# A pooling, convolution and attention trunk on TensorE: three groups of side work issued later

## The chip, the cores and the metric

The kernel runs on one core of a Trainium2 chip. The metric is the device time of one execution in microseconds (us). The engines are called as in the profile: PE is TensorE's matrix multiply, DVE is VectorE, ACT is ScalarE, POOL is GpSimd, and SP is SyncE, which here only issues DMAs.

## The reference

Four residual layers with a normalization ahead of each, and a final normalization: pooling, gated convolution, latent attention, pooling. Sequence 512, width 1024, inner width 2048. The parts that the change touches:

```python
# pooling layer: windows 2, 4, 8, 16, one for each quarter of the channels
u, z = jnp.split(xn @ w_in, 2, axis=-1)
mean = (c - prev) / jnp.minimum(count_base, float(w))[None, :, None]   # c: running sum of u
pooled.append(mean - uf[:, :, g])
mixed = jnp.einsum('bsgc,gcd->bsgd', pooled, w_grp).reshape(B, S, D_INNER) * scale
return (mixed * jax.nn.silu(z)) @ w_out

# attention layer, 16 heads: a part of the query is turned by its position
q_rope = apply_rope(q[..., QK_NOPE_DIM:], cos[:, :, None, :], sin[:, :, None, :])
s = (einsum('bqhd,bkhd->bhqk', qn_b, k_nope) + einsum('bqhr,bkr->bhqk', qr_b, k_rope)) * ATTN_SCALE
```

where `apply_rope` makes of two halves x1, x2 the pair x1 cos - x2 sin, x2 cos + x1 sin.

## The kernel before

Activations lie with channels on the partitions and the 512 positions along the free dimension. Every float32 product is formed on PE from high and low parts (h, l) as three matmuls: h·h, h·l, l·h (`mm3`, and the lines L261 to L263). So each weight chunk `wr` that SP loads (128x1024, 512 KB) is converted to `wh` by ACT (L248), and DVE subtracts to get `wl` (L251); activations are split in the same way (`split`, L158 and L161).

Layers 0 to 2 run as a stream of jobs. A job is one weight chunk (24 matmuls of 512 columns) or a *pair* of chunks, which is formed by seven half-size products with sums of weights and sums of activations (`seven`, L423 and L429). For a pair, `prepare_pair` makes on ACT and DVE the parts ah/al, sh/sl, ch/cl and, after two more sums (L402, L403), th/tl. The matching sums of the normalized activations are the *forms* of `XNorm.forms`: for each two of the eight x tiles, ACT makes g, DVE four sums d (L366 to L369), ACT two conversions fh, DVE two subtractions fl (L385). Jobs of a layer come in the order of `ORDER`: u, z and m with a group and a number (u12 is the chunk 2 of group 1 that gives u), h0 and h1 the two halves of the output projection. In the pooling layers u and m jobs are chunks; of the z jobs, those of group 0 of layer 0 are two chunks each (z00a, z00b), the others are pairs. In layer 0, z10 is the first pair, and so the first to read forms.

Work other than matmuls is put into a table of positions: eight positions make one job, and a step at position p is issued between the matmuls of that eighth of the job. The table orders PE, DVE and ACT in the program's own order; POOL and the DMA queues follow the program's order too. The last pooling layer and the heads of attention are not placed by such a table: there a scheduler at build time orders the engines.

For u, `post_u` puts at position 0 a multiplication by the normalization's factor (u, L583) and on POOL one to four shifted additions (s, L620), at 12 the mean on DVE (L626 to L628: hd, s, s), at 14 the high part `plh` on ACT (L631), at 16 the low part `pll` on DVE (L634). The multiplied, gated result of m is E and O or sz (L664), split into yh and yl (L667, L670).

In attention a head h passes `scores` (PE s, L1021 to L1025; DVE a masked maximum, L1029; ACT the exponential, L1033; DVE the reciprocal; POOL p times it, L1035), then the next head's query and key projection (pq, pk and their splits q, k), the mixing of head h-1 with the values (po, O or E), and `turn_p`, which transposes p on PE (pj, L1048) and splits it (th, tl, L1051). The turned queries are made for a group of four heads at once: `qrope` projects two halves A and B, does six DVE operations (L985 to L990), splits the two results (qa, qb), and spreads them by 16 DMAs on SP over four tiles `qrs` (L996), one for each head. `extra` is called at five places of a head and issues the next group's values and rotary work at the (head in the group, place) of `VALUES_AT` and `ROTARY_AT`.

Nearly all 128x512 tiles come from one ring of 70 slots (`ut`, NU = 70); a new tile takes the slot of the one 70 before it and waits for its readers, DMAs included. PSUM has eight banks, taken in a ring as well (`ps`).

Of the kernel before, what the change touches and what calls it, by code (L numbers as in the profile page):

```python
# [13 lines left out]
ALU = mybir.AluOpType  # L14
# [27 lines left out]


VALUES_AT = ((0, 3), (2, 0), (2, 0))
ROTARY_AT = ((2, 1), (1, 1), (1, 1))
SPLIT_Y_FROM = 10


# [16 lines left out]
def trunk_kernel(ctx: ExitStack, tc: tile.TileContext, a):  # L65
    nc = tc.nc
# [12 lines left out]
    def ut(s, dt=F32, w=S):  # L79
        return up.tile([P, S + PAD], dt, tag="u", name=nm(s))[:, :w]  # L80
# [74 lines left out]
    def split(src, s, eng="act", w=S):  # L155
        h, l = ut(s + "h", F32R, w), ut(s + "l", F32R, w)
        if eng == "act":
            nc.scalar.activation(h, src, AF.Copy)  # L158
        else:
            nc.vector.tensor_copy(h, src)  # L160
        nc.vector.tensor_tensor(out=l, in0=src, in1=f(h), op=ALU.subtract)  # L161
        return h, l
# [92 lines left out]
    def wchunk(src, width=CH, pool=False):  # L255
        w, steps = prepare_chunk(load_chunk(src, width)[0], width, pool)
        Steps(steps)(2)
        return w
# [323 lines left out]
    def tmul(dst, src, R):  # L582
# [1 line left out]


    LATE = "u20 u21 m10 u22 u23 m11 h0 z20 z21 u30 u31 m20 u32 u33 m21 z30 z31 m30 m31 h1"
    ORDER = ("u00 u01 u02 u03 u10 u11 u12 u13 z00 z01 m00 m01 z10 z11 " + LATE,
             "u00 u01 u02 u03 z00 z01 u10 u11 m00 u12 u13 m01 z10 z11 " + LATE)

    def pool_layer(stream, j, xn, half, mid=None, at=(1, 3), pre=None):  # L590
# [12 lines left out]
        for g, w in enumerate(WINDOWS):  # L603
            pooled, szs = [], []

            def post_u(t, sign, g=g, w=w, pooled=pooled):
                u = up.tile([P, S + PAD], F32, tag="u", name=nm("u"))
                h, l = ut("plh", F32R), ut("pll", F32R)
                pooled.append((h, l))
                sums = []  # L610

                def mul():
                    nc.gpsimd.memset(u[:, :PAD], 0.0)
                    tmul(u[:, PAD:], t, ly.R[sign])
                    sums.append(u)

                def add(d):
                    cur, nx = sums[0], up.tile([P, S + PAD], F32, tag="u", name=nm("s"))
                    lo = 2 * d - 1
                    nc.gpsimd.tensor_tensor(out=nx[:, lo:], in0=cur[:, lo:], in1=cur[:, lo - d : S + PAD - d], op=ALU.add)  # L620
                    sums[0] = nx

                def mean():
                    cur, pd = sums[0], sums[0][:, PAD:]
                    hd = sp.tile([P, PAD], F32, tag="hd", name=nm("hd"))
                    nc.vector.tensor_tensor(out=hd, in0=cur[:, PAD : 2 * PAD], in1=con[:, C_INV + PAD * g : C_INV + PAD * (g + 1)], op=ALU.mult)  # L626
                    nc.vector.scalar_tensor_tensor(out=pd, in0=cur[:, PAD:], scalar=1.0 / w, in1=u[:, PAD:], op0=ALU.mult, op1=ALU.subtract)
                    nc.vector.tensor_tensor(out=pd[:, :PAD], in0=hd, in1=u[:, PAD : 2 * PAD], op=ALU.subtract)  # L628

                def high():  # L630
                    nc.scalar.activation(h, sums[0][:, PAD:], AF.Copy)  # L631

                def low():
                    nc.vector.tensor_tensor(out=l, in0=sums[0][:, PAD:], in1=f(h), op=ALU.subtract)  # L634

                adds = [lambda q=q: add(2**q) for q in range(g + 1)]
                return {0: [mul, *adds], 12: [mean], 14: [high], 16: [low]}

            def post_z(t, sign, szs=szs, plain=g == 0 and pre is not None):
                sz = ut("sz") if plain else t  # L640

                def scale():
                    tmul(sz, t, ly.R[sign])

                def gate():
                    nc.scalar.activation(sz, sz, AF.Silu)
                    szs.append(sz)

                return {0: [scale], 3: [gate]}

            def mix(mm, g=g, pooled=pooled, szs=szs):
                def run(wl, now):
                    for e in range(2):
                        i = 2 * mm + e
                        pm = ps("pm")
                        for k in range(4):
                            now(4 * e + k)
                            c = slice(k * 2 * P + e * P, k * 2 * P + (e + 1) * P)
                            mm3(pm, wl[0][:, c], wl[1][:, c], *pooled[k], first=k == 0, last=k == 3)
                        y, h, l = szs[i], ut("yh", F32R), ut("yl", F32R)  # L660
                        ys[g // 2].append((h, l))

                        def gated(pm=pm, y=y, i=i):
                            nc.vector.scalar_tensor_tensor(out=y, in0=pm, scalar=pcol(f"pool_scale{j}", 4 * g + i), in1=y, op0=ALU.mult, op1=ALU.mult)  # L664

                        def high(h=h, y=y):
                            nc.scalar.activation(h, y, AF.Copy)  # L667

                        def low(h=h, l=l, y=y):
                            nc.vector.tensor_tensor(out=l, in0=y, in1=f(h), op=ALU.subtract)  # L670

                        (stream.later if e else now).put({0: [gated], 3: [high], 4: [low]} if e else {5: [gated], 6: [high], 7: [low]})

                stream.add(CHUNK, wg[g, mm], run)

            for i in range(4):
                u_[g, i] = lambda g=g, i=i, post_u=post_u: ly.tile(stream, wu[4 * g + i], post_u)
            for i in range(2):
                z_[g, i] = lambda g=g, i=i, post_z=post_z: (ly.pair if g or pre is None else two_tiles)(stream, wz[2 * g + i], (post_z, post_z), mid and mid(g, i))
                m_[g, i] = lambda mix=mix, i=i: mix(i)  # L680
            if g == 0 and pre is not None:
                u_[0, 0] = lambda post_u=post_u: stream.add(None, None, lambda w, now: ly.done(stream, *[(post_u, t, 1) for t in pre()]))
                u_[0, 1] = lambda: None
# [115 lines left out]
    def mla_layer(stream, xn, begin, cos_sin, nxt):  # L799
# [161 lines left out]
        def values(g):  # L961
            wh, wl = wchunk(wv[g])
            for tk in range(NT):
# [7 lines left out]
                    nc.tensor.matmul(pv, xl[:, ts_], wh[:, c], start=False, stop=(k == 1))  # L971
                vs[g, tk] = split(pv, "v")

        def qrope(g):
            wh, wl = wchunk(wq[8 + g], 768)
            ab = []
            for e in range(2):
                pa = ps("pa")
                mtile(pa, wh, wl, ql, kn=3, ktot=3, stride=2 * P, off=e * P)
                t = ut("qr")  # L980
                nc.scalar.activation(t, pa, AF.Copy)
                ab.append(t)
            A, B = ab
            t1, t2 = ut("t1"), ut("t2")
            nc.vector.tensor_tensor(out=t1, in0=A, in1=cos, op=ALU.mult)  # L985
            nc.vector.tensor_tensor(out=t2, in0=B, in1=sin, op=ALU.mult)
            nc.vector.tensor_tensor(out=t1, in0=t1, in1=t2, op=ALU.subtract)
            nc.vector.tensor_tensor(out=t2, in0=B, in1=cos, op=ALU.mult)
            nc.vector.tensor_tensor(out=A, in0=A, in1=sin, op=ALU.mult)
            nc.vector.tensor_tensor(out=t2, in0=t2, in1=A, op=ALU.add)  # L990
            parts = [*split(t1, "qa"), *split(t2, "qb")]
            order = [parts[0], parts[2], parts[1], parts[3]]
            for hh in range(4):
                st = ut("qrs", F32R)
                for q, src in enumerate(order):
                    nc.sync.dma_start(f(st)[32 * q : 32 * q + 32, :], f(src)[32 * hh : 32 * hh + 32, :])  # L996
                qrs[4 * g + hh] = st
# [74 lines left out]
        cos, sin = cos_sin  # L1072
        for h in range(H):
            g, e = divmod(h, 4)

            def extra(pos):
                if g < 3:
                    if (e, pos) == VALUES_AT[g]:
                        values(g + 1)
                    if (e, pos) == ROTARY_AT[g]:  # L1080
                        qrope(g + 1)

            extra(0)
            scores(h)
            extra(1)
            if h + 1 < H:
                stage_a(h + 1)
            extra(2)
            if h:
                mix(h - 1)  # L1090
            extra(3)
            if h >= SPLIT_Y_FROM:
                for _ in range(2):
                    split_y()
            if h + 1 == H:
                nxt.begin()
                nxt.step()
            turn_p(h)
            extra(4)
# [23 lines left out]
    def first_two():  # L1123
# [32 lines left out]
            s1.later.put({0: [lambda m=m: xn0.st.add(xt[m])]})  # L1156
        s1.later.put({3: [xn0.st.close]})
        for kk in range(KK):
            s1.later.put(xn0.forms(kk), 48 + 8 * kk)
        return pre  # L1160

    pool_layer(s1, 0, xn0, half, at=(3, 5), pre=first_two)
# [221 lines left out]
```

## Time and profile before

| | us |
|---|---|
| median of three runs | 1491.59 |
| lowest and highest run | 1488.02 and 1491.71 |
| the profiled execution | 1488.14 |
| its span, first to last instruction | 1486.4 |
| PE busy | 1442.5 |
| DVE busy | 1090.3 |
| ACT busy | 685.1 |
| POOL busy | 254.7 |

The mean clock that was granted to TensorE over the span is 0.992 of full speed. The profile's page gives the busy time of each engine; the list of waits gives, for each engine and line, what ended its idle time; the windows give busy time and clock of a stretch; the timeline gives rows in order of time, with the idle time ahead of a row and what ended it in square brackets. In such a row the first number is the start in us, the second the duration; a row with xN joins N instructions of one form.

### The profile page before, as it was taken

How to read it: one execution, taken by the hardware profiler on the slowest of the kernel's cores; microseconds unless marked ns; L12 is line 12 of the kernel's file. 1: busy time of each engine (PE TensorE's matmuls, PEld its weight loads, DVE VectorE, ACT ScalarE, POOL GpSimd, SP SyncE). 2: the span in 40 equal slices, each digit the busy share in tenths (PEclk: the TensorE clock that was granted, in tenths of full speed). 3: DMA queues.
4: the chain of work that ended last, by engine and by line, in shares of the span. 5: the costliest groups of instructions: out<-in, count | busy, mean ns of one | idle time of the engine just before them, and what ended most of it. 6: DMA issues, size and time to landing. Idle time of an engine off the chain costs nothing. (4 is left out here: it accounts for less than half of the span.)

```text
span 1486.4 us, 22441 instructions
## 1 busy us (share of the span) xinstructions
PE 1442.5 (97%) x8560; PEld 1271.0 (86%) x8560; DVE 1090.3 (73%) x1771; ACT 685.1 (46%) x1174; POOL 254.7 (17%) x291
## 2 busy tenths in 40 slices
PE   9899998999999999999999999999999999999898
PEld 6688797987999889999879987888888898888786
DVE  6885556749999879999688977677755588655773
ACT  4353242435555426555355655555633355323352
POOL 3402206021001000010211001111201132310502
PEclk9999999999999999999999999999999999999999
DMA  6143344425777357776236742122122443343431
GB/s 231 57 121 121 101 127 99 142 75 123 178 185 192 129 135 184 187 183 177 93 97 170 169 137 82 44 69 85 44 85 85 114 128 97 131 114 107 119 114 57
DMA packets 65147, 181.71 MB, mean 122 GB/s; under 512 B 8080, under 2 KB 8080, under 8 KB 65040
## 3 DMA queue, kind: packets, MB, share of 16 engines
q1 hardware_dynamic: 56688, 151.44, 33.4%
q0 software_dynamic: 7488, 27.27, 10.7%
q10 hardware_dynamic: 864, 1.57, 0.3%
q8 instruction: 67, 1.10, 0.3%
q14 instruction: 40, 0.33, 0.1%
HBM read 173.70 MB, written 2.10 MB: 118 GB/s over the span
## 5 line engine op out<-in xcount | busy, mean ns | idle before, releaser
L251 DVE TENSOR_TENSOR wl<-wr,wh 128x1024 fp32r<-128x1024 f32 (+1 forms) x140 | 173.3, 1238 | 52.5 <-ACT wh L248 52.0
L248 ACT ACTIVATE wh<-wr 128x1024 fp32r<-128x1024 f32 (+1 forms) x140 | 144.4, 1034 | 139.6 <-PE o L262 47.7
L263 PE MATMUL o<-yh,wl 128*128 128x512 f32 x384 | 151.1, 394 | 1.9 <-DVE wl L251 1.9
L262 PE MATMUL o<-yl,wh 128*128 128x512 f32 x384 | 151.2, 394 | 0.2 <-DVE yl L670 0.2
L261 PE MATMUL pt<-xh,wh 128*128 128x512 f32 x367 | 145.9, 398 | 5.6 <-ACT wh L248 5.2
L261 PE MATMUL o<-yh,wh 128*128 128x512 f32 x384 | 151.2, 394 | 0.1
L263 PE MATMUL pt<-xh,wl 128*128 128x512 f32 x367 | 145.1, 396 | 4.0 <-DVE wl L251 3.9
L262 PE MATMUL pt<-xl,wh 128*128 128x512 f32 x367 | 145.4, 396 | 1.0 <-DVE xl L352 0.9
L443 ACT ACTIVATE kept<-bv 128x256 f32<-128x256 f32 x52 | 19.9, 382 | 169.5 <-PE bv L429 137.4
L263 PEld LDWEIGHTS o<-yh,wl 128*128 128x128 f32 x384 | 72.1, 188 | 19.4 <-DVE wl L251 2.8
L261 PEld LDWEIGHTS pt<-xh,wh 128*128 128x128 f32 x367 | 69.4, 189 | 22.3 <-ACT wh L248 6.1
L263 PEld LDWEIGHTS pt<-xh,wl 128*128 128x128 f32 x367 | 69.3, 189 | 22.4 <-DVE wl L251 6.9
L262 PEld LDWEIGHTS o<-yl,wh 128*128 128x128 f32 x384 | 72.2, 188 | 17.1 <-DVE yl L670 0.5
L261 PEld LDWEIGHTS o<-yh,wh 128*128 128x128 f32 x384 | 72.0, 188 | 16.9 <-ACT yh L667 0.5
L262 PEld LDWEIGHTS pt<-xl,wh 128*128 128x128 f32 x367 | 69.5, 189 | 17.8 <-DVE xl L352 2.6
L399 DVE TENSOR_TENSOR sl<-s,sh 128x1024 fp32r<-128x1024 f32 x52 | 64.6, 1242 | 22.1 <-ACT sh L396 22.1
L121 POOL DMA_DIRECT2D s<-in_conv_in x30 | 26.0, 866 | 310.0 <-DMA s<-in_conv_in 95.4
L285 POOL TENSOR_TENSOR sq<-sq,sq 128x512 f32<-128x512 f32 x25 | 41.2, 1649 | 203.4 <-ACT sq L279 203.1
L399 DVE TENSOR_TENSOR al<-wr,ah 128x1024 fp32r<-128x1024 f32 x52 | 64.2, 1234 | 15.4 <-ACT ah L396 13.4
L620 POOL TENSOR_TENSOR s<-u 128x527 f32<-128x527 f32 x32 | 48.9, 1527 | 154.3 <-DVE u L583 146.1
L620 POOL TENSOR_TENSOR s<-s 128x525 f32<-128x525 f32 (+2 forms) x48 | 66.1, 1377 | 14.5 <-PE pm L262 11.2
L443 ACT ACTIVATE kept<-bx 128x512 f32<-128x512 f32 x104 | 50.9, 490 | 37.1 <-PE bx L429 37.1
(308 smaller groups left out, 4576.2 us busy)
## 6 DMA issues: line engine op xcount, KB each, us to landing
wr<-in_conv_in SPq DMA_DIRECT2D x34, 512.0 KB, 4.5
wr<-in_pool_out SPq DMA_DIRECT2D x32, 512.0 KB, 3.3
wr<-in_pool_u SPq DMA_DIRECT2D x30, 512.0 KB, 3.5
s<-in_conv_in SPq DMA_DIRECT2D x60, 256.0 KB, 3.9
s<-in_conv_in POOLq DMA_DIRECT2D x30, 512.0 KB, 7.0
wr<-in_pool_z SPq DMA_DIRECT2D x18, 512.0 KB, 4.5
wr<-in_pool_grp SPq DMA_DIRECT2D x16, 512.0 KB, 3.4
wr<-in_conv_out SPq DMA_DIRECT2D x16, 512.0 KB, 3.3
```

What stands on the lines that cost most here:

```text
L121: return (r, r4, s13), {4: [lambda: nc.gpsimd.dma_start(s13, src[:, :CH], accum_op=ALU.add)]}
L248: nc.scalar.activation(h, raw, AF.Copy)
L251: (nc.gpsimd if pool else nc.vector).tensor_tensor(out=l, in0=raw, in1=f(h), op=ALU.subtract)
L261: nc.tensor.matmul(out, ah, bh, start=first, stop=False)
L262: nc.tensor.matmul(out, ah, bl, start=False, stop=False)
L263: nc.tensor.matmul(out, al, bh, start=False, stop=last)
L285: eng.tensor_tensor(out=self.sum, in0=self.sum, in1=sq, op=ALU.add)
L399: return lambda: nc.vector.tensor_tensor(out=l, in0=t, in1=f(h), op=ALU.subtract)
L443: nc.scalar.activation(dst, src, AF.Copy)
L620: nc.gpsimd.tensor_tensor(out=nx[:, lo:], in0=cur[:, lo:], in1=cur[:, lo - d : S + PAD - d], op=ALU.add)
```

## The change

Four things are moved; the operations are the same, but for the tiles: the second turned half writes one product into A's tile instead of a t2 of its own.

1. The forms of layer 0 are put 16 positions (two jobs) later: the first pair of x tiles at position 64 instead of 48, and so on.
2. In layer 0's order, u20 and u21 come ahead of z10 and z11, and m10 after them. The last pooling layer's order is as it was.
3. Mean, high part and low part of groups 2 and 3 (windows 8 and 16) come six positions later, in both pooling layers.
4. `qrope` is cut into four calls: the projection with its copies (`qrope`), the first turned half with its split (`qturn(0)`), the second with its split (`qturn(1)`), and the 16 DMAs (`qspread`), over two heads.

```diff
-ROTARY_AT = ((2, 1), (1, 1), (1, 1))
+ROTARY_AT = (((2, 1), (2, 3), (3, 1), (3, 1)), ((1, 1), (1, 3), (2, 1), (2, 1)), ((1, 1), (1, 3), (2, 1), (2, 1)))
...
-    ORDER = ("u00 u01 u02 u03 u10 u11 u12 u13 z00 z01 m00 m01 z10 z11 " + LATE,
+    ORDER = ("u00 u01 u02 u03 u10 u11 u12 u13 z00 z01 m00 m01 u20 u21 z10 z11 m10 u22 u23 m11 h0 z20 z21 u30 u31 m20 u32 u33 m21 z30 z31 m30 m31 h1",
              "u00 u01 u02 u03 z00 z01 u10 u11 m00 u12 u13 m01 z10 z11 " + LATE)
...
-                return {0: [mul, *adds], 12: [mean], 14: [high], 16: [low]}
+
+                late = 6 * (g // 2)
+                return {0: [mul, *adds], 12 + late: [mean], 14 + late: [high], 16 + late: [low]}
...
+        def qturn(q):
+
+            A, B = rot["ab"]
+            t, t2 = ut("t1"), ut("t2") if q == 0 else A
+            first, second, op = ((cos, sin, ALU.subtract), (sin, cos, ALU.add))[q]
+            nc.vector.tensor_tensor(out=t, in0=B, in1=second, op=ALU.mult)
+            nc.vector.tensor_tensor(out=t2, in0=A, in1=first, op=ALU.mult)
+            nc.vector.tensor_tensor(out=t, in0=t2, in1=t, op=op)
+            rot[q] = split(t, "qab"[::2][q])
+
+        def qspread(g):
+            order = [rot[q][n] for n in range(2) for q in range(2)]
             for hh in range(4):
                 st = ut("qrs", F32R)
                 for q, src in enumerate(order):
...
-                    if (e, pos) == ROTARY_AT[g]:
-                        qrope(g + 1)
+                    for at, fn in zip(ROTARY_AT[g], (lambda: qrope(g + 1), lambda: qturn(0), lambda: qturn(1), lambda: qspread(g + 1))):
+                        if (e, pos) == at:
+                            fn()
...
-            s1.later.put(xn0.forms(kk), 48 + 8 * kk)
+            s1.later.put(xn0.forms(kk), 64 + 8 * kk)
```

How the order on DVE moves, at three places. The rows give the line, the operation, the tile written and the tiles read. First the start of layer 0, behind the weight split wl_549. The mean on s_516 is that of u13, `plh`/`pll` are the parts of a finished mean, d and fl are the forms. Before:

```order
L366 SCALAR_TENSOR_TENSOR d_137_582<-x_72,par,g_572 128x256
L367 SCALAR_TENSOR_TENSOR d_137_582<-x_73,par,g_572 128x256
L368 SCALAR_TENSOR_TENSOR d_138_583<-x_73,npar,d_137_582 128x256
L369 SCALAR_TENSOR_TENSOR d_138_583<-x_73,npar,d_138_583 128x256
L634 TENSOR_TENSOR pll_392<-s_472,plh_391 128x512
L626 TENSOR_TENSOR hd_592<-s_500,con 128x16
L627 SCALAR_TENSOR_TENSOR s_500<-s_500,u_487 128x512
L628 TENSOR_TENSOR s_500<-hd_592,u_487 128x16
L385 TENSOR_TENSOR fl_600<-d_137_582,fh_599 128x512
L385 TENSOR_TENSOR fl_603<-d_138_583,fh_602 128x512
L626 TENSOR_TENSOR hd_610<-s_516,con 128x16
L627 SCALAR_TENSOR_TENSOR s_516<-s_516,u_393 128x512
```

After:

```order
L634 TENSOR_TENSOR pll_392<-s_472,plh_391 128x512
L626 TENSOR_TENSOR hd_584<-s_500,con 128x16
L627 SCALAR_TENSOR_TENSOR s_500<-s_500,u_487 128x512
L628 TENSOR_TENSOR s_500<-hd_584,u_487 128x16
L626 TENSOR_TENSOR hd_594<-s_516,con 128x16
L627 SCALAR_TENSOR_TENSOR s_516<-s_516,u_393 128x512
L628 TENSOR_TENSOR s_516<-hd_594,u_393 128x16
L634 TENSOR_TENSOR pll_489<-s_500,plh_488 128x512
L583 TENSOR_TENSOR sz_605<-pt_550,R_380 128x512
L251 TENSOR_TENSOR wl_609<-wr_546,wh_608 128x1024
```

The four sums and the two fl have left this place; the two means follow each other. The forms now stand from two jobs further on.

Second, layer 0 at z30, where PE uses al, sl, cl and tl of this pair in turn and the mean is that of u32. Here u_2132 is the multiplication for u33. Before, the rows from there:

```order
L583 TENSOR_TENSOR u_2132<-pt_2093,R_380 128x512
L626 TENSOR_TENSOR hd_2177<-s_2103,con 128x16
L627 SCALAR_TENSOR_TENSOR s_2103<-s_2103,u_2081 128x512
L628 TENSOR_TENSOR s_2103<-hd_2177,u_2081 128x16
L399 TENSOR_TENSOR al_2143<-wr_2087,ah_2142 128x1024
L664 SCALAR_TENSOR_TENSOR E_1803<-pm_2150,par,E_1803 128x512
L399 TENSOR_TENSOR sl_2147<-s_400_2084,sh_2146 128x1024
L399 TENSOR_TENSOR cl_2145<-wq_2088,ch_2144 128x512
L402 TENSOR_TENSOR wr_2087<-s_400_2084,wr_2087 128x512
L403 TENSOR_TENSOR wq_2088<-wr_2087,wq_2088 128x512
```

After (the mean on s_2097 is u32's here):

```order
L583 TENSOR_TENSOR u_2132<-pt_2088,R_380 128x512
L399 TENSOR_TENSOR al_2143<-wr_2082,ah_2142 128x1024
L666 SCALAR_TENSOR_TENSOR E_1803<-pm_2150,par,E_1803 128x512
L399 TENSOR_TENSOR sl_2147<-s_399_2079,sh_2146 128x1024
L399 TENSOR_TENSOR cl_2145<-wq_2083,ch_2144 128x512
L402 TENSOR_TENSOR wr_2082<-s_399_2079,wr_2082 128x512
L403 TENSOR_TENSOR wq_2083<-wr_2082,wq_2083 128x512
L672 TENSOR_TENSOR yl_2174<-E_1803,yh_2173 128x512
L666 SCALAR_TENSOR_TENSOR O_1804<-pm_2175,par,O_1804 128x512
L626 TENSOR_TENSOR hd_2245<-s_2097,con 128x16
L627 SCALAR_TENSOR_TENSOR s_2097<-s_2097,u_2076 128x512
L628 TENSOR_TENSOR s_2097<-hd_2245,u_2076 128x16
```

al, sl, cl and the two sums of weights now stand ahead of the mean of u32, which has moved to just ahead of tl.

Third, attention while heads 10 and 11 pass, for the queries of the last group. Before, while head 9 passes:

```order
L985 TENSOR_TENSOR t_1951_10614<-qr_10600,cos 128x512
L989 TENSOR_TENSOR qr_10600<-qr_10600,sin 128x512
L251 TENSOR_TENSOR wl_10725<-wr_10722,wh_10724 128x1024
L986 TENSOR_TENSOR t_1952_10615<-qr_10612,sin 128x512
L987 TENSOR_TENSOR t_1951_10614<-t_1951_10614,t_1952_10615 128x512
L988 TENSOR_TENSOR t_1952_10615<-qr_10612,cos 128x512
L161 TENSOR_TENSOR qal_10623<-t_1951_10614,qah_10622 128x512
L990 TENSOR_TENSOR t_1952_10615<-t_1952_10615,qr_10600 128x512
L1063 TENSOR_TENSOR E_8603<-po_10681,E_8603 128x512
L161 TENSOR_TENSOR qbl_10627<-t_1952_10615,qbh_10626 128x512
```

After, the second half alone stands in head 10's part, behind the masked maxima and among the reciprocals (the row of its first multiplication lies three rows above these):

```order
L1043 RECIPROCAL sm_10757<-sm_10757 128x1
L1043 RECIPROCAL sm_10769<-sm_10769 128x1
L997 TENSOR_TENSOR t_2006_10798<-qr_10602,t_2006_10798 128x512
L1043 RECIPROCAL sm_10781<-sm_10781 128x1
L1043 RECIPROCAL sm_10793<-sm_10793 128x1
L251 TENSOR_TENSOR wl_10960<-wr_10957,wh_10959 128x1024
L161 TENSOR_TENSOR bl_10803<-t_2006_10798,bh_10802 128x512
L251 TENSOR_TENSOR wl_11216<-wr_11213,wh_11215 128x768
L1072 TENSOR_TENSOR O_8604<-po_10851,O_8604 128x512
L161 TENSOR_TENSOR ql_10837<-pq_10826,qh_10836 128x512
L161 TENSOR_TENSOR kl_10848<-pk_10840,kh_10847 128x512
L1078 TENSOR_TENSOR yl_10866<-E_8007,yh_10865 128x512
```

The last sum of the second half (L997) and its split bl stand behind head 10's softmax, ahead of ql and kl of head 11 and of tl of head 10.

More of the change, by code (lines that the diff above doesn't have):

```diff
@@ L972, in values @@
                 vs[g, tk] = split(pv, "v")
+        rot = {}
         def qrope(g):
@@ L982, in qrope @@
                 ab.append(t)
[L983 to L992, printed above, removed]
+            rot["ab"] = ab
+        def qturn(q):
[8 more added lines that the diff above has]
+            order = [rot[q][n] for n in range(2) for q in range(2)]
             for hh in range(4):
```

## Prediction

> **What bounds the kernel now.** I read the page's busy times first, then the waits of TensorE, then the clock by windows, and then the rows around each long wait. The page:
>
> ```profile
> PE 1442.5 (97%) x8560; PEld 1271.0 (86%) x8560; DVE 1090.3 (73%) x1771; ACT 685.1 (46%) x1174; POOL 254.7 (17%) x291
> ```
>
> TensorE (PE) is busy 1442.5 of the span's 1486.4 us and its matmuls are the same before and after, so a gain can come only from its 43.9 us of idle time, or from the stretches where its clock drops. The waits of TensorE name the idle pieces (total us, times, longest):
>
> ```profile
> PE pt L261 <- ACT wh L248: 5.2, 2, 4.3
> PE bx L429 <- DVE al L399: 4.7, 2, 3.7
> PE bx L429 <- DVE tl L399: 4.4, 4, 1.9
> PE s L1021 <- ACT kh L158: 4.3, 2, 3.3
> PE pt L263 <- DVE wl L251: 3.9, 5, 1.4
> PE s L1022 <- DVE kl L161: 2.2, 3, 1.0
> PE pj L1048 <- POOL p L1035: 2.2, 1, 2.2
> PE o L263 <- DVE wl L251: 1.9, 2, 1.2
> PE bx L423 <- ACT kept L443: 1.5, 2, 1.2
> ```
>
> Five pieces stand out: 4.3, 3.7, 3.3, 2.2 and 1.9. The windows right behind them, with a quiet stretch last, show busy us of PE, PEld, DVE, ACT, POOL, then the granted clock:
>
> ```profile
> 70.25:77.10 6.85, 4.90 (x11) 3.41 (x12) 6.20 (x14) 4.08 (x7) 0.00 (x0) 0.50 0.27 70
> 257.90:261.40 3.50, 3.50 (x18) 3.27 (x17) 3.46 (x4) 0.32 (x1) 2.06 (x1) 0.51 0.00 0
> 923.55:927.00 3.45, 3.44 (x9) 2.93 (x10) 2.50 (x6) 1.27 (x4) 0.00 (x0) 0.51 0.43 104
> 937.20:940.65 3.45, 3.45 (x12) 2.99 (x11) 2.59 (x7) 0.97 (x4) 0.00 (x0) 0.51 0.00 0
> 1408.30:1411.70 3.40, 3.21 (x15) 3.21 (x16) 3.33 (x7) 1.82 (x4) 0.00 (x0) 0.50 0.51 154
> 100.00:150.00 50.00, 50.00 (x293) 43.99 (x292) 30.98 (x44) 19.22 (x29) 11.20 (x10) 1.00 0.35 116
> ```
>
> Each long wait is followed by half clock. In a 3.4 us window half of the work is lost: 3.4 x 0.5 = 1.7 us; behind the first wait TensorE works 4.90 us at half clock, so 2.45 us. A stall therefore costs its idle time and 1.7 to 2.45 us more.
>
> **1. The first layer's forms (16 positions, two jobs, later).** DVE at the first wait, then ACT and POOL:
>
> ```profile
> 62.38 1.28 DVE L366 SCALAR_TENSOR_TENSOR d<-x,par,g 128x256 f32<-128x256 f32 x1
> 63.58 1.28 DVE L367 SCALAR_TENSOR_TENSOR d<-x,par,g 128x256 f32<-128x256 f32 x1
> 64.79 1.28 DVE L368 SCALAR_TENSOR_TENSOR d<-x,npar,d 128x256 f32<-128x256 f32 x1
> 66.10 0.48 DVE L369 SCALAR_TENSOR_TENSOR d<-x,npar,d 128x256 f32<-128x256 f32 x1
> ...
> 68.13 1.28 DVE L385 TENSOR_TENSOR fl<-d,fh 128x512 fp32r<-128x512 f32 x2
> ```
>
> ```profile
> 70.53 0.63 ACT L631 ACTIVATE plh<-s 128x512 fp32r<-128x512 f32 x1 [1.59 <-DVE s L628]
> 71.06 1.04 ACT L248 ACTIVATE wh<-wr 128x1024 fp32r<-128x1024 f32 x1
> ```
>
> ```profile
> 64.66 1.12 POOL L620 TENSOR_TENSOR s<-s 128x525 f32<-128x525 f32 x1
> ```
>
> The sums hold DVE for 66.50 - 62.38 = 4.1 us and the two fl for 1.2, ahead of the mean of u13. ACT's plh waits for that mean, wh stands behind plh on ACT, and TensorE waits for wh (4.3). Without those 5.3 us the mean could end near 65.2, but its last POOL add ends at 64.66 + 1.12 = 65.8; a mean of some 1.0, plh 0.6 and wh 1.0 then end at 68.4, against TensorE's want at 72.1 - 4.3 = 67.8. Left: about 0.6, no drop. Gain 4.3 - 0.6 + 2.45 = 6.1; the wl wait behind it (in the 3.9 of the fifth row) gives perhaps 0.2: I take 6.3. Ends: 3 (1.9 us of idle stay and one window drops) and 7.7 (all of it).
>
> Per pair of x tiles the forms are four sums, two fl and three ACT operations; they land where z01 to m01 run. DVE there gets 4 x 0.48 + 1.2 = 3.1 us a job, on jobs like those of the quiet stretch, where DVE is busy 30.98 of 50 us (3.4 of 5.5): cost 0, since the first reader, z10, is still two jobs behind. Without that slack DVE runs over by up to 1 us a job. The forms issue no DMA. The new order also puts u20 and u21 ahead of z10: their weight loads pass z10's on SP, a load being
>
> ```profile
> wr<-in_pool_u SPq DMA_DIRECT2D x30, 512.0 KB, 3.5
> ```
>
> 3.5 us to land, issued two jobs ahead: 0 (with that cover gone, 3.5). POOL's adds of u20 now lie beside DVE's preparation of z10. In the rows above DVE's sums took 1.28 instead of 0.48 beside POOL's adds, 0.8 each; I take -0.3, ends -3.7 (the al wait of the second row once more) and 0.
>
> The Trainium skill, SBUF — State Buffer, "Who interferes with whom", says that a DVE operation with two SBUF inputs and a GpSimd operation that reads SBUF exclude each other for the whole instruction. That agrees with 1.28 against 0.48 here, and it speaks against moving u20's adds beside z10; what I charge for it is -0.3.
>
> **2. Means of groups 2 and 3, six positions later.** In layer 0 this puts the weight split wl ahead of the means in the first half of the output projection (the 1.9 row): I take +1.2, ends 0 and 1.9. At z30 of layer 0:
>
> ```profile
> 253.03 0.18 DVE L626 TENSOR_TENSOR hd<-s,con 128x16 f32<-128x16 f32 x1 [4.85 <-POOL u L613]
> 253.25 1.49 DVE L627 SCALAR_TENSOR_TENSOR s<-s,u 128x512 f32<-128x512 f32 x1
> 254.77 0.92 DVE L628 TENSOR_TENSOR s<-hd,u 128x16 f32<-128x16 f32 x1
> 255.61 1.21 DVE L399 TENSOR_TENSOR al<-wr,ah 128x1024 fp32r<-128x1024 f32 x1
> ```
>
> DVE idles 4.85 us for POOL's adds, then does the mean (255.6 - 253.0 = 2.6 us), and only then al, for which TensorE has waited 3.7. In the new order al stands before the mean, so it can run inside those 4.85 us. Gain 3.7 + 1.7 = 5.4; the mean now stands before tl, where I leave 0.8: +4.6. Ends 2.0 (a tl wait takes its place and the clock drops) and 5.4.
>
> At z30 of the last pool layer, which the scheduler orders:
>
> ```profile
> 1400.35 1.50 DVE L627 SCALAR_TENSOR_TENSOR s<-s,u 128x512 f32<-128x512 f32 x1
> ```
>
> ```profile
> 1403.46 0.39 PE L429 MATMUL bv<-xh,cl 128*128 128x256 f32 x1 [0.97 <-DVE cl L399]
> ```
>
> Behind this mean come three waits, 0.97 (cl), 1.2 (kept) and 1.9 (tl), and a drop of 1.7: 5.8 us. The new order keeps the mean of u32 ahead of cl, but issues its multiplication before al and the second mean well after tl; the chain starts some 2 us earlier, by the 0.68-us operations and the second mean it passes. That takes the 0.97 and most of the 1.2 and keeps the last wait under the drop: +3.5. Ends 0 (the scheduler's order only trades one mean for the other) and 5.8.
>
> **3. Rotary in three parts.** Same 6 DVE operations, 2 splits and 16 DMAs per group, for groups 1 to 3. Rows:
>
> ```profile
> 936.05 1.31 PE L1048 MATMUL pj<-con,p 128*128 128x128 f32 x10 [2.15 <-POOL p L1035]
> ```
>
> ```profile
> 931.92 0.69 DVE L1029 CUSTOM_DVE_ANT_0 p<-s,con 128x512 f32<-128x512 f32 x1 [5.87 <-DMA qrs<-qah]
> ```
>
> ```profile
> 1030.88 1.35 DVE L1051 TENSOR_TENSOR tl<-pj,th 128x512 fp32r<-128x512 f32 x3
> ```
>
> ```profile
> 1032.04 0.45 PE L261 MATMUL pq<-lnh,wh 128*128 128x512 f32 x1
> ```
>
> ```profile
> 1024.80 1.04 ACT L248 ACTIVATE wh<-wr 128x1024 fp32r<-128x1024 f32 x1
> ```
>
> ```profile
> L996 SPq DMA_DIRECT2D qrs<-qah x12: 512/531/889, 919.9 to 1019.1; - x12
> L996 SPq DMA_DIRECT2D qrs<-qbl x12: 542/588/589, 923.8 to 1020.9; - x12
> ```
>
> ```profile
> DMA to landing us min/median/max: 1.9/2.0/4.4
> ```
>
> Group 1 (910 to 941) costs 3.3 + 1.7 at the scores, because eight DVE operations and two ACT conversions stand ahead of kh, and 2.15 + 1.7 at the turn, because the masked maximum (L1029) waits 5.87 us for a slot of the common ring that the spread's DMAs still read: 8.9 in all. With half of the burst gone ahead of kh I leave 1.2 at the scores of the two heads, 0.8 at the turn, and 2.0 for the next head's query projection and small splits: 4.0, gain +5. Ends 0 and 8.9. Group 2 costs a kh wait of 4.3 - 3.3 = 1.0; its queries get two more operations ahead: -0.5, ends -4 and +1.0.
>
> Group 3 goes the other way. Its second turn now follows head 10's softmax, and on ACT the conversion bh stands behind wh (24.80 + 1.04 = 1025.8, a little less if the heads before lose nothing). SP issues in order, so DMAs 2 to 16 follow at about 0.6 each: number 13 at 1025.5 + 11 x 0.6 = 1032.1, landed at 1034.1. In the new order the slot that it reads is the one into which tl of head 10 (1030.88 before) is written, and that tl frees a PSUM bank for the query projection of head 12. TensorE, which began that projection at 1032.04, would wait 1034.6 - 1032.0, about 2.6, and 0.3 to 0.5 at the scores; a drop of 1.7 may follow, for 2.15 brought one at 936.05. Before it was 1.0 (the kl wait): -3.5, ends -6 and +1.0.
>
> The Trainium skill, TensorE: Matmul & The Clock Gate, Part 1, gives an idle window of about 3.4 us as what halves the clock. Here 2.15 and 1.9 sufficed, so the measurement decides; by the page group 3 would cost 1.7 less than by the trace, at most.
>
> **Sum.** 6.3 - 0.3 + 1.2 + 4.6 + 3.5 + 5.0 - 0.5 - 3.5 = 16.3. The profiled execution took 1488.14 us (span 1486.4): 1471.8. Two of the three runs shown lie 3.5 above it, and the median is one of them; I put the new median between, 1473.
>
> **Rivals.**
> - *The spread finds its slots free* (15%): group 3 loses nothing, if ACT reaches bh some 3 us earlier than I have it. For it: the DMAs land in 2.0; against: SP's issue pace of 0.6 x 11. 1473 - 4 = 1469.
> - *All stalls of the five places go* (12%): 7.7 + 1.9 + 5.4 + 5.8 + 8.9 + 2.0 = 31.7, less what waits next, some 6: 1488 - 26 + 1.5, about 1463. Against it: POOL's adds end at 65.8 whatever DVE does.
> - *Pool adds block z10* (12%): DVE's al waits as at z30 before, 3.7 + 1.7 = 5.4, instead of 0.3: 1478.
> - *Stalls only move* (12%): the means before tl, the forms in m00/m01 and the spread's slots each bring back an idle over 1.9 with its drop; gains left 3 + 0 + 2.0 + 0 + 0, less 2: about 1487, no measurable change.
> - *Slower* (5%): the slots that the spread's DMAs read hold two heads of every group, not one. A group then costs 8.9 + 3.85; three cost 38, against 8.9 + 1.0 + 1.0 before, a loss of 27 against gains of 15.6 outside attention: about 1500. It decides once the three groups cost over 31 us. For it: every DMA now issues later in its head; against: before, the same slots held DVE long in group 1 alone.
>
> **How the numbers follow.** My forecast has the other 44%: 1473, itself 1467 to 1480 by the ends of terms that are independent. To hold 8 in 10 the range takes in the second and third rival and most of "only move": 1462 to 1486. A run is told from no change here at about 0.3%, 4.5 us. Faster than 1487: the forecast, the first three rivals, and a third of the fourth less what spills over, 0.84; within 0.3%: 0.11; slower: 0.05.
>
> **What would show it.** In the new profile the wh wait of 4.3 and the al wait of 3.7 are gone from TensorE's list, and the windows at 70 and 258 run at clock 1.00; the 1.9 tl wait near 1400 is under 1.2; the kh wait falls from 3.3 to under 1; near 1017 to 1022 (the same place, some 15 earlier) a wait of pq or of pj of 2 to 3 us stands behind DVE's tl, which names a DMA qrs. The prediction is wrong if z10 (about 95) shows an al or tl wait over 2, if half-clock windows stay at three or more places, or if the kh wait only turns into waits for kl of the same sum.

## The result, and the profile after

| | us |
|---|---|
| before, median of four runs beside the change | 1489.88 (1488.02 to 1491.71) |
| after, median of four runs | 1478.63 (1477.62 to 1480.56) |
| ratio, 95% interval | 0.9926 (0.9914 to 0.9939) |
| the profiled execution before, after | 1488.14, 1480.56 |

The change makes the kernel 11 us faster. The profiled execution of after is its slowest, so the two profiles stand only 7.6 us apart, and the terms below are read from them. The page after, and TensorE's waits (total us, times, longest):

```profile
PE 1439.9 (97%) x8560; PEld 1271.6 (86%) x8560; DVE 1094.2 (74%) x1771; ACT 684.6 (46%) x1174; POOL 264.8 (18%) x291
```

```profile
PE pq L261 <- DVE tl L1060: 4.8, 2, 3.6
PE bx L423 <- ACT kept L443: 4.3, 4, 2.8
PE pj L1057 <- POOL p L1044: 4.3, 5, 1.3
PE bx L429 <- DVE tl L399: 3.7, 4, 1.2
PE pt L263 <- DVE wl L251: 3.1, 4, 1.4
PE pt L261 <- ACT wh L248: 2.3, 2, 1.5
```

Of the five long waits of before (4.3, 3.7, 3.3, 2.2, 1.9) none is left at its length. New ones stand at the head of the list: 3.6 for a pq behind tl, in attention, and 2.8 for `kept` (ACT's copy of a partial product out of PSUM), in the last pooling layer. The windows at half clock (the granted clock is the third number from the end) are still at four places:

```profile
70.85:74.20 3.35, 3.35 (x9) 2.63 (x8) 3.05 (x8) 1.86 (x3) 0.00 (x0) 0.50 0.49 159
255.15:258.55 3.40, 3.40 (x19) 3.40 (x18) 2.64 (x4) 1.85 (x3) 0.00 (x0) 0.50 0.65 224
1019.75:1026.55 6.80, 5.16 (x12) 4.12 (x13) 4.18 (x17) 3.83 (x12) 1.88 (x4) 0.50 0.59 192
1398.65:1405.40 6.75, 5.55 (x26) 5.56 (x27) 4.43 (x6) 4.94 (x8) 0.00 (x0) 0.50 0.23 78
```

They are the start of layer 0, z30 of layer 0, the third group's spread, and z30 of the last layer. The first two places have shorter waits than before. The third group's is new; at z30 of the last layer the waits are as long as before (4.02 and 4.05 in sum), with one more window at half clock. At z30 of layer 0, three DVE rows before, then DVE and POOL after:

```profile
258.74 1.76 DVE L399 TENSOR_TENSOR cl<-wq,ch 128x512 fp32r<-128x512 f32 x1
260.43 0.68 DVE L402 TENSOR_TENSOR wr<-s,wr 128x512 f32<-128x512 f32 x1
261.14 0.69 DVE L403 TENSOR_TENSOR wq<-wr,wq 128x512 f32<-128x512 f32 x1
```

```profile
246.41 1.55 DVE L399 TENSOR_TENSOR cl<-wq,ch 128x512 fp32r<-128x512 f32 x1
247.88 1.54 DVE L402 TENSOR_TENSOR wr<-s,wr 128x512 f32<-128x512 f32 x1
249.45 1.67 DVE L403 TENSOR_TENSOR wq<-wr,wq 128x512 f32<-128x512 f32 x1
```

```profile
243.53 1.88 POOL L620 TENSOR_TENSOR s<-u 128x527 f32<-128x527 f32 x1
245.48 5.09 POOL L620 TENSOR_TENSOR s<-s 128x525 f32<-128x525 f32 x3
```

The mean no longer holds al. Before, POOL's four additions of u33 already ran beside cl, which took 1.76 us, and ended ahead of the two sums of weights (0.68 and 0.69); now they run beside all three, which take 1.5 to 1.7 us each. In attention the third group's spread holds a slot:

```profile
1018.49 0.59 SPq L1005 DMA_DIRECT2D qrs<-qh  x1
```

```profile
1020.56 0.69 DVE L1060 TENSOR_TENSOR tl<-pj,th 128x512 fp32r<-128x512 f32 x1 [4.56 <-DMA qrs<-qh]
```

```profile
1021.39 0.77 PE L261 MATMUL pq<-lnh,wh 128*128 128x512 f32 x1 [3.65 <-DVE tl L1060]
```

The 13th DMA is issued at 1018.5 and lands some 2 us later; DVE's tl starts then, after 4.56 us of idleness, and TensorE after 3.65.

### The profile page after: what moved, and what is told of

Its sections match the earlier page's. It is cut to its first block, busy times and chain, and to the rows that moved or that the text cites. A ratio compares the mean times of both kernels' runs of the same rounds, so it can differ in the third digit from the quotient of the medians.

```text
span 1478.8 us, 22407 instructions
## 1 busy us (share of the span) xinstructions
PE 1439.9 (97%) x8560; PEld 1271.6 (86%) x8560; DVE 1094.2 (74%) x1771; ACT 684.6 (46%) x1174; POOL 264.8 (18%) x291
## 5 line engine op out<-in xcount | busy, mean ns | idle before, releaser
L1044 POOL TENSOR_SCALAR p<-p,sm 128x512 f32<-128x512 f32 (+1 forms) x64 | 38.5, 619 | 193.0 <-DVE sm L1043 140.3
L620 POOL TENSOR_TENSOR s<-s 128x525 f32<-128x525 f32 (+2 forms) x48 | 70.5, 1468 | 9.6 <-PE pm L262 6.1
```

The source lines that it names most:

```text
L1044: nc.gpsimd.tensor_scalar(out=pt[:, :w], in0=pt[:, :w], scalar1=sm_, scalar2=1.0, op0=ALU.mult, op1=ALU.mult)
```

## The experiments

Each kernel is the changed one (1478.63) with the edit named; the time given is the median of its runs beside runs of the kernel before (medians 1488.5 to 1489.4), with the ratio's interval.

**rot_back: the four rotary calls at one place.**

```diff
-ROTARY_AT = (((2, 1), (2, 3), (3, 1), (3, 1)), ((1, 1), (1, 3), (2, 1), (2, 1)), ((1, 1), (1, 3), (2, 1), (2, 1)))
+ROTARY_AT = (((2, 1),) * 4, ((1, 1),) * 4, ((1, 1),) * 4)
```

> The four rotary calls of each group stand at one place again, as before the change; the rest of the change stays. Theory: in the profiles TensorE's waits and half-clock losses in attention add up to about 11 us before (group 1: 3.34 + 2.15 + 2 x 1.7; groups 2 and 3 about 1 each) and about 12 after (group 3 alone 0.89 + 3.65 + 3.4), so the rotary part is worth nothing or a little less: 1477 to 1479, against 1478.6 for the changed kernel. Rival, the prediction's sum: it is worth +1.0 net, 1479.6; rival that it carries the result: over 1483.

Measured: 1481.37, 0.9949 (0.9935 to 0.9964), 2.7 slower than the change. That fits none of the three forecasts. In its profile the last rotary sum of the third group (L997) starts at 1003.31, 5.8 us behind the start of the copy of B (997.52, ACT L986); before, it was 4.0 (1010.68 and 1006.69). The row here, then the one before:

```profile
1003.31 0.68 DVE L997 TENSOR_TENSOR t<-qr,t 128x512 f32<-128x512 f32 x1
```

```profile
1010.68 0.68 DVE L990 TENSOR_TENSOR t<-t,qr 128x512 f32<-128x512 f32 x1
```

`qturn` forms B's product first, and DVE waits for B with A's products behind it; before, both of A's products ran while B was still being projected. So the change also altered the order of the products. It takes one tile more for each group, too, a second t1; that one product goes into A's tile is no difference, since the code before did the same (L989). The comparison therefore did not undo the part alone.

**rot_code_back: the rotary code of before** (`qrope` undivided, called at the old places).

> The rotary code of before, word for word, in the changed kernel. It differs from the kernel whose four calls stand at one place (1481.4) only in the order of the products: A's two products run before B's copy is there, and one tile more is taken. Theory: in that kernel the last sum of groups 2 and 3 ended 1.8 us later against the same copy, because B's product stood first, so the product order costs up to 1.8 per group: 1477 to 1478.5 here, and no pj wait of 1.0 in groups 2 and 3. Rival: the order of the products is hidden, 1481 again, and the parts are worth 2.8 net.

Measured: 1478.59, 0.9923 (0.9907 to 0.9940). Against rot_back the old code gives back 2.8; against the change, nothing. The last sum again starts 4.0 us behind the start of B's copy (1002.99 and 999.00), and the pj waits of rot_back in groups 2 and 3 (1.30 and 1.00) are gone, so the order of the products is the likely cause; no run separates it from the tile more. Over all three groups the three parts bring nothing that can be told.

**late_first: late means in layer 0 alone.**

```diff
-                late = 6 * (g // 2)
+                late = 6 * (g // 2) if j == 0 else 0
```

> Late means only in layer 0; the last pooling layer has its means where they were. Theory: the two profiles keep their distance through the last pooling layer to 0.2 us (the waits of 0.97, 1.16 and 1.92 with one half-clock window became 1.18 and 2.84 with two), so undoing this part moves nothing: 1478 to 1479.5. Rival, the prediction's term: it is worth 3.5, so the time goes to 1482.

Measured: 1479.52, 0.9938 (0.9921 to 0.9954). In the last pooling layer the late means bring nothing that can be told.

**forms_back: forms at position 48 and the old order of layer 0.**

> Forms of layer 0 at their old positions and u20, u21 behind z11 again; late means and rotary parts stay. Theory: the profiles part by 4.2 us up to the first output projection, so the time goes to about 1482.8, with the wh wait of 4.3 and a drop of two windows back at 70 us. Rival, the prediction's term of 6.3 - 0.3: 1484.6.

Measured: 1487.0 (1481.72 to 1490.10 in ten runs), 0.9981 (0.9967 to 0.9996). The wait is back:

```profile
PE pt L261 <- ACT wh L248: 5.1, 2, 4.3
```

The spread of the runs follows the clock: the mean granted clock is 0.996 in the fastest and 0.990 in the slowest. The forms and the order together are the largest part undone, 8.4 by the medians, 2.4 between the two profiled spans (1481.2 and 1478.8); it cannot be said more narrowly. At the same matmul near 145 us the two profiles stand 4.2 apart. No run undoes the forms, the order, or the late means of layer 0 alone.

**rot_mix: only the first group in parts.**

```diff
+ROTARY_AT = (((2, 1), (2, 3), (3, 1), (3, 1)), ((1, 1),) * 4, ((1, 1),) * 4)
```

> Only the first group's rotary work in parts, those of groups 2 and 3 at one place as before. Theory: the parts save 8.9 - 2.6 = 6.3 in group 1 and cost 1 in group 2 and 7 in group 3, where DVE's tl waits 4.56 for the DMA that reads its slot and TensorE 3.65, with two windows at half clock. Keeping the one and undoing the others gives 1478.6 - 8 = 1471, and no wait over 1.5 in attention. Rival: the slot's wait is an accident of where the ring stands and comes back at another head: 1476 or more, with a wait on a DMA qrs elsewhere.

Measured: 1477.47, 0.9922 (0.9907 to 0.9937): 1.2 faster, not 8, and by the intervals not told from the change. The 3.65 is gone, as expected, but groups 2 and 3 at one place each have a pj wait of about 1.0, which rot_code_back has not, and a kl wait of 1.0, which stood there before, too; and the losses at half clock were overrated: in the 6.8 us at 1019.75 TensorE was at work for 5.16, so 2.6 were lost, not 3.4.

**spread_by_part: the 16 DMAs of a group by source, not by head.**

```diff
-            for hh in range(4):
-                st = ut("qrs", F32R)
-                for q, src in enumerate(order):
+            sts = [ut("qrs", F32R) for _ in range(4)]
+            for q, src in enumerate(order):
+                for hh in range(4):
```

> The changed kernel, with the 16 DMAs of a group issued by source (all four heads of the first part, then of the second) and not by head, so that the first source's slot comes free after the 4th DMA instead of the 13th. Theory: DVE's tl of head 10 then waits for nothing, the wait of 3.65 and the half clock behind it go: 1478.6 - 6 = 1472 to 1473. Rival: the last four DMAs end as late as before and hold the masked maximum of head 11 instead, so a pj wait of 2 to 3 comes in its place: 1476 or more.

Measured: 1477.34, 0.9918 (0.9904 to 0.9933). The third group's wait went; a new one came in the first group, with half clock behind it:

```profile
934.18 2.18 PE L1058 MATMUL pj<-con,p 128*128 128x128 f32 x9 [4.08 <-POOL p L1045]
```

The rows there show no wait for a slot. By source, the first head's tile of turned queries is complete only with the 13th DMA (issued at 923.67, landed at 925.6), and in the first group that head's scores follow directly; in groups 2 and 3 the spread is issued a head earlier. The build-time scheduler, probably for that reason, puts those of the head's products that read qrs behind po: they start at 928.67, and not at 923.71 as in the changed kernel, and the masked maximum, exponential and transposition follow late. First spread_by_part, then the changed kernel:

```profile
928.67 0.44 PE L1034 MATMUL s<-krh,qrs 128*128 128x512 f32 x1
```

```profile
923.71 0.40 PE L1033 MATMUL s<-krh,qrs 128*128 128x512 f32 x1
```

**spread_mixed: by head in the first group, by source in the other two.**

> The changed kernel; the DMAs of the first group's spread go by head as in it, those of groups 2 and 3 by source. Theory: going by source took away group 3's wait of 3.65 and its drop, but brought a pj wait of 4.08 and two windows of half clock to group 1, where another reader comes 70 tiles later. With each group in its better order both are gone: 1478.6 - 6 = 1472 to 1473, no wait over 1.5 in attention, no half clock between 300 and 1390. Rival: a slot that is held in group 3 in one order or another, the wait moves to head 11 or 12: 1476 or more.

Measured: 1472.25 (1470.30 to 1473.30), 0.9894 (0.9877 to 0.9910), 6.4 faster than the change, and its profile has no half clock in attention. With spread_by_part this settles the third group: its wait is that for a slot which the spread's DMAs still read, and the order of the same 16 DMAs takes it away. The theory's other half, that the first group's wait of 4.08 was a slot's, is not what the rows show; there the products that read the spread's own tile came late.

**adds_out: POOL's additions of group 3 cut from four to one** (the means of window 16 are wrong).

> Three of the four POOL additions of each tile of group 3 are left out, in both pooling layers, so those means are wrong. Theory: in the changed kernel these additions lie beside the preparation of z30, whose DVE operations took 1.4 to 1.75 us instead of 0.6 to 1.2, and that is why kept, th and tl come late (1.04 + 1.24 and 1.18 + 2.84, each with half clock). Without them these waits fall under 0.5: 1478.6 - 7 = 1471.5. Rival: the chain on DVE and ACT is too long without any collision, the waits stay: 1477 or more.

Measured: 1470.89 (1469.14 to 1473.67), 0.9876 (0.9861 to 0.9891). The same rows of DVE at z30, without POOL beside them:

```profile
243.64 0.68 DVE L399 TENSOR_TENSOR cl<-wq,ch 128x512 fp32r<-128x512 f32 x1
244.24 0.69 DVE L402 TENSOR_TENSOR wr<-s,wr 128x512 f32<-128x512 f32 x1
244.96 0.69 DVE L403 TENSOR_TENSOR wq<-wr,wq 128x512 f32<-128x512 f32 x1
```

0.69 instead of 1.5 to 1.7, and no half clock at either z30. The three additions left out of each of the four tiles, in both layers, cost 7.7 us in the changed kernel.

**u3_together: u32 and u33 ahead of m20 in layer 0.**

> In layer 0, u32 and u33 come ahead of m20, so that POOL's additions of group 3 are over sooner, most of them before z30 is prepared. Theory (POOL's additions beside z30 are what is left there): the waits of 1.04 and 1.24 and their drop go, -3 to -4: 1475. Rival: the additions only meet other DVE work, the weight splits and means of m20 and m21, which are waited for as well: 1478 or more.

Measured: 1479.55 (1478.42 to 1482.96), 0.9936 (0.9921 to 0.9951), no gain. Earlier additions met other operations: its profile has an al wait of 1.75 near 248 instead.

**last_adds_dve: u33's additions on DVE, ahead of tl of z31.**

> In both pooling layers the four additions of u33 are done by DVE behind tl of z30, and not by POOL beside z30's preparation. Theory: leaving POOL's additions out took 7.7; u33's are the ones beside z30, so most of it comes back with the sums right: DVE's cl, wr and wq at 0.6 to 0.7 us, kept and tl waits under 0.6, no half clock at z30: 1478.6 - 5 = 1473 to 1474. Rival: DVE's four additions, 2.6 us, delay z31's tl or the next weight split by as much: 1477 or more.

Measured: 1477.63 (1475.58 to 1480.62), 0.9929 (0.9912 to 0.9946). z30 is as forecast, but the rival came true as well: the additions stand just ahead of z31's tl, in both layers.

```profile
260.91 1.43 DVE L620 TENSOR_TENSOR s<-s 128x521 f32<-128x521 f32 x2
262.25 0.68 DVE L399 TENSOR_TENSOR tl<-wr,th 128x512 fp32r<-128x512 f32 x1
```

```profile
262.99 0.38 PE L429 MATMUL bx<-fh,tl 128*128 128x256 f32 x1 [2.17 <-DVE tl L399]
```

**filled: TensorE kept busy with zero weights where it waits for kept.**

```diff
+        for _ in range(fill):          # 9 in layer 0, 23 in the last pooling layer, at z30
+            nc.tensor.matmul(Z, zero, xf[0]["B22"][0], start=False, stop=False, skip_group_check=True)
         product(w, xf, "S2", "N2", X)
```

> At z30 of both pooling layers TensorE runs matmuls with a zero weight tile (9 and 23 of 256 columns, 0.117 us each, adding nothing) at the place where it waits for kept, 1.04 and 2.84 us. Nothing else is made faster. Theory: half clock follows from idle time summed within a window of 3.4 us, so with the wait filled the clock stays at 1.00 at both places and the time falls by the loss of these windows, 1.7 and about 2.5: 1478.6 - 4 = 1474.5, with DVE's and ACT's rows as before. Rival: the drop does not hang on idle time, or the zero matmuls delay the real ones: 1478 or more, clock 0.5 still there.

Measured: 1477.07 (1476.64 to 1478.38), 0.9925 (0.9910 to 0.9940). The clock did what was expected at both places, with DVE no faster:

```profile
251.70:258.50 6.80, 5.69 (x49) 5.49 (x48) 6.17 (x11) 4.72 (x8) 0.00 (x0) 1.00 0.44 152
1393.60:1401.00 7.40, 7.29 (x59) 7.09 (x60) 6.31 (x6) 4.27 (x8) 2.47 (x2) 1.00 0.30 105
```

The time fell by 1.6 and not by 4. Set matmul against matmul, the two profiles tell where the rest went. From the wait of z30 to the last matmuls of the next pair, z31, that come ahead of its tl, `filled` gains 1.9 us on the changed kernel in layer 0 (from 0.59 behind it to 1.33 ahead) and 2.5 in the last layer (1.96 to 4.42 ahead), so the windows are worth about what was expected. Then 0.8 and 0.9 are lost again, most of it in waits for z31's tl, which the changed kernel does not have:

```profile
264.94 0.39 PE L431 MATMUL bx<-fh,tl 128*128 128x256 f32 x1 [0.49 <-DVE tl L401]
1408.92 0.39 PE L431 MATMUL bx<-fh,tl 128*128 128x256 f32 x1 [0.62 <-DVE tl L401]
```

With full clock TensorE comes to z31's tl earlier than DVE has it. Of the 2.7 that are left in these two profiles the medians show 1.6; that difference no run explains.

**best: spread_mixed, and u33's additions on DVE behind tl of z31.**

```diff
+                if dve:                # u33 alone
+                    return {0: [mul], 20: adds, 21: [mean], 23: [high], 24: [low]}
```

> Two edits together: the spread's order by group (by head in the first, by source in the other two, alone 1472.25), and u33's four additions on DVE in both pooling layers, now behind tl of z31 instead of ahead of it, where they had made a tl wait of 2.17. Theory: with the additions out of both ways the waits of z30 (0.46 + 1.24, 0.90 + 2.86 with half clock) fall under 0.6 each and z31's tl stays under 0.6: 1472.3 - 4.5 = 1467.5 to 1468.5, with half clock at most at one place between 100 and 1460. Rival: the mean of u33 then comes too late for the last matmuls of m30, a wait on pll or plh of 1 to 2 in both layers: 1470 or more.

Measured: 1465.37 (1465.04 to 1466.83), 0.9842 (0.9828 to 0.9855), 13 faster than the change and faster than forecast. Its longest waits:

```profile
PE pj L1060 <- POOL p L1047: 3.2, 4, 0.9
PE pt L263 <- DVE wl L251: 3.1, 4, 1.4
PE bx L429 <- DVE tl L399: 3.0, 4, 1.0
PE pt L261 <- ACT wh L248: 2.3, 2, 1.4
```

The rival's wait on pll exists (0.64 in each layer) and costs less than what it replaces. Between 76 and 1460 us its profile has no half clock.

## Why the prediction was right, and where it was wrong

The direction and the range held, the mechanism only in part. The waits of 4.31 (wh), 3.67 (al) and 3.34 (kh) went, and the third group lost by the DMA, the tile and the wait that were named. But the windows near 70 and 258, forecast at full clock, are at half, and half clock stays at four places; three or more were among the prediction's own signs of being wrong. The forecast of 1473 was 5.6 too low, and its sum of 16.3 stands against 11.2 by the medians and 7.6 between the profiles. That the total lies in the range owes much to the range's width, 24 us.

By the start of the same matmul in both profiles, the change gains 4.3 us at the forms, 2.3 in the first half of the output projection, 0.7 more by 235 us and 1.5 at z30 of layer 0. In attention it gains 5.4 in group 1 and loses 0.7 in group 2 and 5.8 in group 3, and at z30 of the last layer it loses 0.6; the rest is drift of less than half a microsecond between these places. Term by term:

- *Forms, +6.3.* Idle before 4.31 + 0.99 and 2.45 at half clock; after 1.45 + 0.53 and 1.7. Right in mechanism, mis-sized: about 4.1. The step that failed is the end of the mean. I let POOL's last addition end at 65.8 and took 1.0 for the mean; without the forms, other two-input DVE work met that addition, which took 1.60 instead of 1.12 and ended at 66.25 (64.65 + 1.60). Only then the mean of u13 ran, in 1.1 us. With that plh and wh came 0.6 later than forecast, and TensorE wanted wh 0.2 sooner. TensorE waits for wh until 69.03. The wl wait behind it, 0.53, was enough to bring the drop that I had left out.

```profile
64.65 1.60 POOL L620 TENSOR_TENSOR s<-s 128x525 f32<-128x525 f32 x1
```

```profile
69.03 0.50 PE L261 MATMUL pt<-xh,wh 128*128 128x512 f32 x1 [1.45 <-ACT wh L248]
70.29 0.50 PE L263 MATMUL pt<-xh,wl 128*128 128x512 f32 x1 [0.53 <-DVE wl L251]
```

- *u20 beside z10, -0.3.* No wait of 0.25 or more stands between 71 and 148. Right.
- *First half of the output projection, +1.2.* 0.70 + 0.22 + 1.21 became 0.70, by the waits 1.4; by the matmuls 2.3, above the end of 1.9 that I gave it. Right in mechanism.
- *z30 of layer 0, +4.6.* al came early as worked out, its wait of 3.67 went, but the chain behind it gave back 1.04 + 1.24 and a drop: about 1.4 gained. The failed step is "I leave 0.8" at tl: the collision of POOL's additions, which I had priced for z10, was not priced for z30, where the change put them beside the two sums of weights as well. adds_out shows this cause.
- *z30 of the last layer, +3.5.* Nothing (late_first, 1479.52 against 1478.63). 0.97 + 1.16 + 1.92 became 1.18 + 2.84. The step that failed is "the chain starts some 2 us earlier". The multiplication for u32 did come sooner, and POOL's additions of u32 began 9.5 us ahead of TensorE's want of cl instead of 7.9. But with DVE's wr, sl and pll beside them, the last three took 5.09 us instead of 3.57, and other DVE work followed, so the mean began 1.7 ahead of that want; before, it was 2.3. POOL before and after, then a DVE row after:

```profile
1396.53 3.57 POOL L620 TENSOR_TENSOR s<-s 128x525 f32<-128x525 f32 x3
```

```profile
1386.91 5.09 POOL L620 TENSOR_TENSOR s<-s 128x525 f32<-128x525 f32 x3
1396.89 1.75 DVE L403 TENSOR_TENSOR wq<-wr,wq 128x512 f32<-128x512 f32 x1
```

u33's additions then met wq, as in layer 0. It is the same collision, and adds_out takes these waits away, too.

- *Rotary, +5.0 - 0.5 - 3.5.* Group 1 has 1.17 + 0.72 + 0.57 + 0.16 of idle left of 8.9, better than the 4.0 that I left. For group 2 I read the second kh wait of before as its cost; that wait (0.92, at 883.27) stands ahead of group 1, and group 2's own is the kl wait at 979.45 (1.02), of the same size by chance. Group 3 lost as forecast, by the DMA, the tile and the wait named, but with 3.65 for 2.6 and two windows of half clock. The 13th DMA was issued 7.9 us behind the second, where I had 6.6; 0.9 of this is one issue that took 1.50 instead of 0.59:

```profile
1014.41 1.50 SPq L1005 DMA_DIRECT2D qrs<-bl  x1
```

Together nothing (rot_code_back), where I had +1.0. What I had not seen is the new order of the products; with the tile more it costs 2.8 where the calls stand together, and no run prices it where they stand apart.

Of the rivals, the one with POOL's additions came nearest by its time, 1478, and its mechanism is the one found, but at z30 in both layers and not at z10; that the number agrees is chance. "Stalls only move" came true in two of its places, the sums ahead of tl at z30 and the spread's slot in group 3, while the forms kept most of their gain. The slower one, that the slots hold every group, did not come: a held slot cost TensorE 3.65 us in the third group, and no wait of TensorE in the other two is over 1.3.

## What to carry to other kernels

When a stall is taken away by moving work, look at what the moved work now runs beside, on the other engine too: here POOL's additions, which had stretched single operations before, cost 7.7 us beside a whole chain of DVE operations with two inputs. In a batch of DMAs on one queue, a tile that is read comes free only when its last reader has landed (the 13th of 16 here), and a tile that is written is complete only with its last part; the order of the batch decides who waits for which. Reordering the same 16 DMAs in the two groups that have a head to spare was worth 6.4 us, and doing it in the first group too took 5 us of that back. When a part is undone to price it, undo its code as well as its place: rot_back and rot_code_back differ by 2.8. And a wait taken away is worth its full length only up to the next wait behind it, as `filled` shows.

## What the runs showed of the hardware

Over the fourteen profiles, the granted clock changes only on a grid of 3.41 us, whose phase differs from execution to execution. I summed TensorE's idle pieces in each window of that grid. Leaving out the first 10 us and the last 8 us of each execution, all 43 windows at full clock with 1.72 us of idleness or more, about half of the window, were followed by a window at half clock; none with 1.63 or less was, whether the idleness was one wait or three. So two short waits, such as 1.45 and 0.53, can cost a window in one execution and nothing in the next, as the grid falls between them or not (rot_back's profile has the same two waits and full clock there). Once at half clock, less is enough: all 12 windows at half clock with 0.65 us of idleness or more were followed by another, and all 44 with 0.52 or less by full clock. Both can account for much of the spread between runs of one kernel: forms_back's go from 1481.7 at a mean clock of 0.996 to 1490.1 at 0.990. The Trainium skill, TensorE: Matmul & The Clock Gate, Part 1, has the free-running window of about 3.4 us, which the traces confirm; its idle window as the condition is not what they show, since half a window was enough.
